# A linear-attention level issued in six steps instead of five, an unscaled k in its last level, and moving sums on VectorE instead of GpSimd

## Chip, core and metric

The kernel runs on one core of a Trainium2 chip. The metric is the device time of one execution in microseconds (us). Engines are named as in the profile: PE (TensorE), PEld (its weight loads), DVE (VectorE), ACT (ScalarE), POOL (GpSimd), SP (which issues most DMAs). Each engine works through its own instructions strictly in order, and waits at an instruction whose inputs are not there.

## What is computed

Two layers of a diffusion backbone over 128 context tokens and 256 latent tokens (T = 384 columns, features on the partitions). Each layer has a projection, three parallel mixers (A: attention, B: gated linear attention, C: a pooling mixer), three gated branch projections, an output projection, and a feed-forward part. The parts that matter here, cut from the reference:

```python
# B, per chunk of 64 tokens: decays between every pair of positions
diff = b_[:, :, :, None, :] - b_[:, :, None, :, :]
decay = jnp.exp(jnp.where(causal, diff, -jnp.inf))
A = jnp.einsum('bhtd,bhsd,bhtsd->bhts', q_, k_, decay)
...
# C, per group of 128 channels with window w = 2, 4, 8, 16
win_sum = cs[:, hi, gi] - cs[:, lo, gi]
pooled = win_sum / cnt - uf
y = jnp.einsum('btgi,gio->btgo', pooled, w_pool)
```

All of it is float32. A product is made of three passes (high times high, low times high, high times low), so every weight tile is split into `wh` (ACT, L151) and `wl` (DVE, L155).

## The kernel before

**Segments and ticks.** The main line is a list of segments, mostly one weight tile times 24 matmuls (`mm3`, L219) into a PSUM bank of `pd` (three banks), evacuated by ACT. Beside it run Python generators, the threads. A segment ticks twice: in the middle of its matmuls and at its end. At a tick every thread issues its instructions up to its next `yield`, in the order in which the threads were started. A tick is a place in the issue order of each engine, not a time; one segment of 24 matmuls lasts about 4.2 us, so a tick about 2.1 us of PE. After the mid-tick the segment issues the `wl` split (L155) of the tile two segments ahead.

**Order in a layer.** Counting ticks from the end of the last row segment (tick 1), a layer's segments are: `uc` 0 to 3 (ticks 2 to 9: mid and end of each), `ka` (10, 11), `va` (12, 13), `q` 0 to 3 (14 to 21), `vb` 0 to 3 (22 to 29, L1353, three banks of `pd` at once), `rb` 0 to 3 (30 to 37), then the gates and weights of branch c (from 38; L1421 are branch matmuls), a and b. L472 are small modulation matmuls between segments.

**Thread B (`gla`).** It makes the gates at ticks 2 to 5 (L726 to L738) and the diagonal at 6 (L771). Then come seven levels with blocks of B = 128, 64, ..., 2 rows. A level has five things to do: `subs` (four DVE subtractions of 128x384, L787 to L790), `exps` (two ACT exponentials of 128x768, L793), `mults` (two DVE products of 128x768, L797: z = 0 for q, z = 1 for k), `products` (small matmuls L762 or L810) and what takes their result out of PSUM: four DVE copies (L817, level 0), eight ACT copies (L825, level 1), or two predicated DVE copies (L832, later levels). They are issued over five ticks: level 0's `subs` at 7 and `exps` at 8 and 9; then `mults` 0 and `subs` 1 at 11 and 12, `exps` 1 at 13 and 14, `products` 0 at 15; `mults` 1, `subs` 2 at 16 and 17, `exps` 2 at 18 and 19, `products` 1 at 20; and so on to `products` 6 at 42. After that the thread waits for the attention, which ends at tick 63.

**Thread C (`pool_mix`).** It starts at tick 9. Per group g it issues on POOL g + 1 additions (L1151, about 410 columns), two multiplications and two subtractions (L1156, L1157, 128 and 256 columns) into the one buffer `pl`, yields four times, and issues the matmul L1161 that reads `pl`, its two evacuations (L1163 ACT, L1164 DVE), and yields again. So the matmuls of groups 0 to 3 stand at ticks 13, 18, 23 and 28. POOL does not wait for ticks and runs ahead up to the reuse of `pl`.

**Thread A (`attn`).** It starts at tick 21; its scores (L1066, DVE L1070 to L1074, ACT L1082 and L1083, DVE L1089 to L1091, transposes L1101, PSUM evacuation L1102, L1112) are issued from tick 33 on. All three threads take their PSUM banks in turn out of four (`psa`); a pair of scores holds two of them until the next tick.

Of the kernel before, what the change touches and what calls it, by code (L numbers as in the profile page):

```python
# [10 lines left out]
AF = mybir.ActivationFunctionType  # L11
ALU = mybir.AluOpType
# [11 lines left out]
LEVELS = (128, 64, 32, 16, 8, 4, 2)  # L24
# [6 lines left out]
class Kern:  # L31
# [683 lines left out]
    def gla_gates(self, l, gl, wg):  # L715
# [3 lines left out]
        yield  # L719
        E = self.mid(8, [128, 4, T])  # L720
        N = self.mid(9, [128, 4, T])
        for q in range(4):
# [4 lines left out]
            b = self.vec[l][:, V_BG + q:V_BG + q + 1]  # L727
            nc.scalar.activation(E[:, q, :], ps, AF.Abs, bias=b)
            nc.vector.tensor_scalar(N[:, q, :], ps, b, 0.0, op0=ALU.add, op1=ALU.min)
# [17 lines left out]
    def gla(self, l, st):  # L747
        nc, P = self.nc, self.P
        qk = st["qbkb"]
        qk2 = qk.rearrange("p (s i) t -> p s (i t)", s=2)  # L750
# [22 lines left out]
        yield  # L773
        lev = {}

        def subs(li):
            B = LEVELS[li]
            W = B // 2
            E = lev[li] = self.mid(8 + li % 2, [128, 2, 768])
            v = lambda x: x.rearrange("p a (n t w) -> p a n t w", t=2, w=W)  # L780
            b = v(P[:, 0:6, 1:129])
            c = v(P[:, 6:12, 0:128])
            rf = b[:, :, :, 0, W - 1:W].to_broadcast([128, 6, 128 // B, W])
            rb = c[:, :, :, 1, 0:1].to_broadcast([128, 6, 128 // B, W])
            qe = v(E[:, 0].rearrange("p (a t) -> p a t", a=6))
            ke = v(E[:, 1].rearrange("p (a t) -> p a t", a=6))
            nc.vector.tensor_tensor(qe[:, :, :, 1], b[:, :, :, 1], rf, op=ALU.subtract)  # L787
            nc.vector.tensor_tensor(ke[:, :, :, 0], rf, b[:, :, :, 0], op=ALU.subtract)
            nc.vector.tensor_tensor(qe[:, :, :, 0], rb, c[:, :, :, 0], op=ALU.subtract)
            nc.vector.tensor_tensor(ke[:, :, :, 1], c[:, :, :, 1], rb, op=ALU.subtract)  # L790

        def exps(li, z):
            nc.scalar.activation(lev[li][:, z], lev[li][:, z], AF.Exp, scale=1.0 / 16)  # L793

        def mults(li):
            for z in range(2):
                nc.vector.tensor_tensor(lev[li][:, z], lev[li][:, z], qk2[:, z], op=ALU.mult)  # L797

        def products(li):
            B = LEVELS[li]  # L800
            E = lev.pop(li)
            Q, K = E[:, 0], E[:, 1]
            if B == 128:
                ps = self.psg()
                for c in range(3):
                    for h in range(4):
                        base = (h // 2) * 384 + c * 128
                        f = (c * 2 + h // 2) * 64
                        for z in range(2):
                            nc.tensor.matmul(  # L810
                                ps[h % 2][64 * z:64 * z + 64, f:f + 64],
                                K[hp(h), base + 64 * z:base + 64 * z + 64],
                                Q[hp(h), base + 64 * (1 - z):base + 64 * (1 - z) + 64],
                                tile_position=(64 * (h % 2), 64 * z))
                for y in range(2):
                    for z in range(2):
                        nc.vector.tensor_copy(  # L817
                            Ap[64 * z:64 * z + 64, y, :, 64 * (1 - z):64 * (1 - z) + 64],
                            ps[y][64 * z:64 * z + 64, 0:384].rearrange("p (a t) -> p a t", t=64))
            elif B == 64:  # L820
                ps = self.psg()
                small(ps, K, Q, True)
                for y in range(2):
                    for j in range(4):
                        nc.scalar.activation(  # L825
                            Ap[32 * j:32 * j + 32, y, :, 32 * (j ^ 1):32 * (j ^ 1) + 32],
                            ps[y][32 * j:32 * j + 32, 0:192].rearrange("p (a t) -> p a t", t=32), AF.Copy)
            else:
                ps = self.psg()
                small(ps, K, Q, False)  # L830
                for z in range(2):
                    nc.vector.copy_predicated(  # L832
                        Dg[:, z * 6:z * 6 + 6], self.masks[:, li - 2].unsqueeze(1).to_broadcast([128, 6, 32]),
                        ps[z][:, 0:192].rearrange("p (a t) -> p a t", t=32))

        NL = len(LEVELS)
        for li in range(NL + 1):
            if li:
                mults(li - 1)
                yield  # L840
            if li < NL:
                subs(li)
                yield
                for z in range(2):
                    exps(li, z)
                    yield
            if li:
                products(li - 1)
            yield
        for j in range(4):  # L850
            nc.vector.tensor_copy(A[32 * j:32 * j + 32, :, 32 * j:32 * j + 32], Dg[32 * j:32 * j + 32])
        while not st.get("attn_done"):
# [39 lines left out]
        for d in range(2):  # L892
            ps = pg[d]
            for n in range(2):
                c = 0 if n == 0 else 1 + d
# [57 lines left out]
        for c in range(3):  # L953
            gc = go[:, c * 4:c * 4 + 4, :]
            nc.vector.tensor_tensor(gc, gc, rs[:, c * 4:c * 4 + 4].unsqueeze(2).to_broadcast([128, 4, 128]),
                                    op=ALU.mult)
# [179 lines left out]
    def pool_mix(self, l, st):  # L1136

        nc = self.nc
        inv = st["inv"]
        wp = st["misc"][:, 512:1024]  # L1140
        och, ocl = st["oc"]
        for g in range(4):
            u = st["uc"][g]
            w = 2 << g
            n = 416
            src = u
            for s in range(g + 1):
                sh = 1 << s
                n -= sh
                dst = st["pw"][s % 2]  # L1150
                nc.gpsimd.tensor_tensor(dst[:, 0:n], src[:, 0:n], src[:, sh:sh + n], op=ALU.add)  # L1151
                src = dst
            pl = self.t("pl", [128, T], bufs=1)
            for (c0, c1), off in zip(SEG, (8, 24)):
                o = off + c0 - w // 2
                nc.gpsimd.tensor_tensor(pl[:, c0:c1], src[:, o:o + c1 - c0], inv[:, g, c0:c1], op=ALU.mult)  # L1156
                nc.gpsimd.tensor_tensor(pl[:, c0:c1], pl[:, c0:c1], u[:, off + c0:off + c1], op=ALU.subtract)  # L1157
            for _ in range(4):
                yield
            ps = self.psa()  # L1160
            nc.tensor.matmul(ps[:, 0:T], wp[:, g * 128:g * 128 + 128], pl)  # L1161
            s = self.vec[l][:, V_PS + g:V_PS + g + 1]
            nc.scalar.activation(och[:, g, :], ps[:, 0:T], AF.Copy, scale=s)  # L1163
            nc.vector.scalar_tensor_tensor(out=ocl[:, g, :], in0=ps[:, 0:T], scalar=s,  # L1164
                                           in1=och[:, g, :].bitcast(F32), op0=ALU.mult, op1=ALU.subtract)
            yield
        st["pool_done"] = True
# [567 lines left out]
```

## Time and profile before

| | us |
|---|---|
| median of 3 runs (1335.37 to 1337.27) | 1336.8 |
| the profiled execution | 1336.65 |
| its span, first to last instruction | 1334.8 |
| around the span | 1.85 |
| PE busy, DVE busy, ACT busy, POOL busy | 1295.1, 857.8, 595.6, 144.4 |
| the B and C threads in layer 0, layer 1 | about 55 to 180, about 711 to 840 |

PE is busy nearly all the time, so only what keeps PE waiting, or slows its clock, counts. The views to read are therefore who PE waited for, then the time lines of the engines around those waits.

### The profile page before, as it was taken

Reading aid. Unit: us, or ns where it says so; the run is one execution under the profiler, and the core shown is the slowest. Engines: PE = TensorE matmul, PEld = TensorE weight load, DVE = VectorE, ACT = ScalarE, POOL = GpSimd, SP = SyncE. Lnnn points to the kernel's source line nnn. Section 1 sums busy time; section 2 is a strip of 40 time slices with the busy share of each in tenths; the row PEclk is TensorE's granted clock in tenths of the full one; section 3 lists DMA queues with packets and bytes.
Section 4 is the critical chain, followed back from the end, with each engine's and each line's share of the span. In section 5 each row is a group of like instructions: output and inputs, shape, how many; then the busy total and the mean of one; then the engine's idle time right before and its main releaser. Section 6 shows DMA issues by size and latency. Waiting matters only on the chain.

```text
span 1334.8 us, 23428 instructions
## 1 busy us (share of the span) xinstructions
PE 1295.1 (97%) x9285; PEld 1201.8 (90%) x9285; DVE 857.8 (64%) x1528; ACT 595.6 (45%) x1104; POOL 144.4 (11%) x190
## 2 busy tenths in 40 slices
PE   7998999999999999999998899999999999999998
PEld 5796788889998999999988777888999899999998
DVE  4497976454568767676877878754556777544432
ACT  5646545343356333332446545543435643333221
POOL 1142000010033000000222500001101300000000
PEclk9999999999999999999999999999999999999999
DMA  9942545557444656565745435456344366444442
GB/s 288 243 113 84 155 120 147 159 135 199 133 126 120 193 168 202 172 204 174 206 133 138 118 97 147 123 149 168 101 124 128 91 190 190 141 127 121 130 131 61
DMA packets 297789, 198.51 MB, mean 149 GB/s; under 512 B 24561, under 2 KB 282385, under 8 KB 297681
## 3 DMA queue, kind: packets, MB, share of 16 engines
q1 hardware_dynamic: 296928, 196.68, 52.3%
q8 instruction: 73, 1.20, 0.4%
q0 software_dynamic: 608, 0.28, 0.1%
q14 instruction: 36, 0.29, 0.1%
q10 hardware_dynamic: 144, 0.07, 0.0%
HBM read 194.64 MB, written 2.36 MB: 148 GB/s over the span
## 4 chain that ended last, share of the span: by engine, by line
PE 81%; DVE 9%; issue 3%; ACT 3%; DMA 2%; SPq 1%; POOL 1%; DVEq 0%; ACTq 0%; POOLq 0%
PE d L219 60%; PE d L1421 8%; DMA m<-in_w_mod_dram 2%; DVE wl L155 2%; PE d L1353 2%; PE m L472 1%; DVE m L797 1%; PE s L1112 1%; PE s L1066 1%; PE s L1101 1%; PE s L941 1%; SPq L1173 1%; DVE ev L656 1%; PE s L935 1%; POOL hl L671 1%
## 5 line engine op out<-in xcount | busy, mean ns | idle before, releaser
L155 DVE TENSOR_TENSOR wl<-raw,wh 128x1024 fp32r<-128x1024 f32 (+2 forms) x274 | 328.6, 1202 | 125.9 <-ACT wh L151 121.6
L151 ACT ACTIVATE wh<-raw 128x1024 fp32r<-128x1024 f32 (+2 forms) x276 | 280.2, 1017 | 173.8 <-PE d L219 63.4
L219 PE MATMUL d<-hh,wh 128*128 128x384 f32 x1248 | 249.3, 343 | 4.0 <-DVE vf L624 2.3
L219 PE MATMUL d<-hl,wh 128*128 128x384 f32 x1248 | 251.2, 340 | 0.0
L219 PE MATMUL d<-hh,wl 128*128 128x384 f32 x1248 | 242.1, 337 | 0.9 <-DVE wl L155 0.8
L219 PEld LDWEIGHTS d<-hh,wh 128*128 128x128 f32 x1248 | 216.9, 189 | 19.9 <-issue 13.9
L219 PEld LDWEIGHTS d<-hh,wl 128*128 128x128 f32 x1248 | 218.4, 188 | 1.9 <-DVE wl L155 1.9
L219 PEld LDWEIGHTS d<-hl,wh 128*128 128x128 f32 x1248 | 217.4, 189 | 1.9 <-issue 0.3
L219 PE MATMUL d<-m,wh 128*128 128x384 f32 x896 | 166.0, 337 | 0.0
L219 PEld LDWEIGHTS d<-m,wh 128*128 128x128 f32 x896 | 155.7, 188 | 0.4 <-issue 0.4
L251 ACT ACTIVATE m<-tt 128x384 fp32r<-128x384 f32 x60 | 31.3, 525 | 157.6 <-DVE tt L1523 125.6
L219 PE MATMUL d<-m,wl 128*128 128x384 f32 x448 | 87.5, 336 | 0.0
L219 PEld LDWEIGHTS d<-m,wl 128*128 128x128 f32 x448 | 78.6, 189 | 0.0
L1421 PE MATMUL d<-m,wh 128*128 128x384 f32 x384 | 72.2, 341 | 0.0
L1421 PEld LDWEIGHTS d<-m,wh 128*128 128x128 f32 x384 | 66.0, 188 | 6.6 <-issue 5.8
L710 DVE SCALAR_TENSOR_TENSOR x<-d,modT,x 128x128 f32<-128x128 f32 x64 | 23.6, 413 | 54.8 <-PE d L219 47.0
L1441 POOL TENSOR_TENSOR m<-m,tt 128x384 f32<-128x384 f32 x16 | 17.0, 1081 | 366.7 <-DVE tt L1439 366.7
L561 POOL TENSOR_TENSOR ssq<-ssq,ev 128x384 f32<-128x384 f32 x18 | 29.5, 1636 | 249.3 <-ACT ev L559 249.3
L1404 ACT ACTIVATE tt<-d 128x384 f32<-128x384 f32 x48 | 23.6, 491 | 70.8 <-PE d L219 60.9
L1523 DVE TENSOR_TENSOR tt<-tt,d 128x384 f32<-128x384 f32 x42 | 23.3, 554 | 48.9 <-PE d L219 48.6
L1510 ACT ACTIVATE tt<-d 128x384 f32<-128x384 f32 x42 | 20.6, 491 | 64.9 <-PE d L219 60.9
L498 DVE SCALAR_TENSOR_TENSOR A<-raw,sc,A 128x1024 f32<-128x1024 f32 x35 | 47.1, 1345 | 0.0
(317 smaller groups left out, 1595.4 us busy)
## 6 DMA issues: line engine op xcount, KB each, us to landing
raw<-in_w_mod_dram SPq DMA_DIRECT2D x80, 512.0 KB, 3.8
raw<-in_w_in_dram SPq DMA_DIRECT2D x76, 512.0 KB, 4.0
raw<-in_w_ff_gate_dram SPq DMA_DIRECT2D x44, 512.0 KB, 4.9
raw<-in_w_ff_up_dram SPq DMA_DIRECT2D x44, 512.0 KB, 4.3
raw<-in_w_ff_down_dram SPq DMA_DIRECT2D x32, 448.0 KB, 4.4
m<-in_w_mod_dram SPq DMA_DIRECT2D x16, 512.0 KB, 6.9
raw<-in_w_in_dram SPq DMA_DIRECT2D x32, 256.0 KB, 3.8
raw<-in_w_out_dram SPq DMA_DIRECT2D x16, 512.0 KB, 4.0
```

The costliest lines, as they stand in the source:

```text
L151: nc.scalar.activation(h[:, f], w[:, f], AF.Copy)
L155: e.tensor_tensor(l[:, f], w[:, f], h[:, f].bitcast(F32), op=ALU.subtract)
L219: nc.tensor.matmul(ps, w[:, k * width + col:k * width + col + 128], xs[xi](k0 + k), start=first and n == 0, stop=last and n == tot - 1)
L251: self.nc.scalar.activation(h, v, AF.Copy)
L498: nc.vector.scalar_tensor_tensor(out=acc, in0=self.raw[u], scalar=s, in1=acc, op0=ALU.mult, op1=ALU.add)
L561: e.tensor_tensor(self.ssq, self.ssq, sq, op=ALU.add)
L710: nc.vector.scalar_tensor_tensor(out=self.x[n][:, c0:c1], in0=ps[:, c0:c1], scalar=self.modT[l][:, fg + n, v:v + 1], in1=self.x[n][:, c0:c ...
L1353: nc.tensor.matmul(vps[c], (self.hl if z else self.hh)[kk][:, c * 128:c * 128 + 128], w[:, k * 512:k * 512 + 512], start=kk == 0 and w is ...
L1404: nc.scalar.activation(tt, ps[:, 0:T], AF.Tanh, scale=0.5)
L1421: nc.tensor.matmul(ps[i], w[:, k * 256 + i * 128:k * 256 + i * 128 + 128], x2[xi](k), start=w is h and xi == 0 and k == 0, stop=w is lo an ...
L1510: nc.scalar.activation(tt, pg, AF.Tanh, scale=0.5)
L1523: nc.vector.tensor_tensor(tt, tt, pu, op=ALU.mult)
```

## The change

The six steps of a level are now: `mults` z = 0, `mults` z = 1, `subs` z = 0, `subs` z = 1 together with the `products` of the level before, `exps` 0, `exps` 1. Each of the two `mults` and the two halves of `subs` has a tick of its own. Level 0 runs over ticks 7 to 10; `products` 0 to 6 stand at ticks 14, 20, 26, 32, 38, 44 and 49. At B = 2 the k side (whose exponent is zero) takes no `subs`, `exps` or `mults`, and `products` reads k as it is. In the pooling thread the additions, multiplications and subtractions go to DVE, with a yield after every second addition and two yields instead of four ahead of the matmul: the matmuls L1161 stand at ticks 11, 15, 19 and 24.

```diff
-        def subs(li):
+        def subs(li, z):
...
-            E = lev[li] = self.mid(8 + li % 2, [128, 2, 768])
+            if z == 0:
+                lev[li] = self.mid(8 + li % 2, [128, 2, 768])
+            elif W == 1:
+                return
...
+            e = v(lev[li][:, z].rearrange("p (a t) -> p a t", a=6))
+            if z == 0:
+                nc.vector.tensor_tensor(e[:, :, :, 1], b[:, :, :, 1], rf, op=ALU.subtract)
+                nc.vector.tensor_tensor(e[:, :, :, 0], rb, c[:, :, :, 0], op=ALU.subtract)
+            else:
+                nc.vector.tensor_tensor(e[:, :, :, 0], rf, b[:, :, :, 0], op=ALU.subtract)
+                nc.vector.tensor_tensor(e[:, :, :, 1], c[:, :, :, 1], rb, op=ALU.subtract)
...
         def exps(li, z):
-            nc.scalar.activation(lev[li][:, z], lev[li][:, z], AF.Exp, scale=1.0 / 16)
-
-        def mults(li):
-            for z in range(2):
+            if z == 0 or LEVELS[li] > 2:
+                nc.scalar.activation(lev[li][:, z], lev[li][:, z], AF.Exp, scale=1.0 / 16)
+
+        def mults(li, z):
+            if z == 0 or LEVELS[li] > 2:
                 nc.vector.tensor_tensor(lev[li][:, z], lev[li][:, z], qk2[:, z], op=ALU.mult)
...
-            Q, K = E[:, 0], E[:, 1]
+            Q, K = E[:, 0], E[:, 1] if B > 2 else qk2[:, 1]
...
         for li in range(NL + 1):
-            if li:
-                mults(li - 1)
+            for z in range(2 if li else 0):
+                mults(li - 1, z)
                 yield
-            if li < NL:
-                subs(li)
+            for z in range(2 if li < NL else 0):
+                subs(li, z)
+                if z:
+                    break
                 yield
-                for z in range(2):
-                    exps(li, z)
-                    yield
             if li:
                 products(li - 1)
             yield
+            for z in range(2 if li < NL else 0):
+                exps(li, z)
+                yield
...
-                nc.gpsimd.tensor_tensor(dst[:, 0:n], src[:, 0:n], src[:, sh:sh + n], op=ALU.add)
+                nc.vector.tensor_tensor(dst[:, 0:n], src[:, 0:n], src[:, sh:sh + n], op=ALU.add)
                 src = dst
+                if s % 2:
+                    yield
...
-                nc.gpsimd.tensor_tensor(pl[:, c0:c1], src[:, o:o + c1 - c0], inv[:, g, c0:c1], op=ALU.mult)
-                nc.gpsimd.tensor_tensor(pl[:, c0:c1], pl[:, c0:c1], u[:, off + c0:off + c1], op=ALU.subtract)
-            for _ in range(4):
+                nc.vector.tensor_tensor(pl[:, c0:c1], src[:, o:o + c1 - c0], inv[:, g, c0:c1], op=ALU.mult)
+                nc.vector.tensor_tensor(pl[:, c0:c1], pl[:, c0:c1], u[:, off + c0:off + c1], op=ALU.subtract)
+            for _ in range(2):
                 yield
```

## Rows read from the trace of the kernel before

**Rows 1.** The page, part 1: busy us (share of the span) and instructions.

```profile
PE 1295.1 (97%) x9285; PEld 1201.8 (90%) x9285; DVE 857.8 (64%) x1528; ACT 595.6 (45%) x1104; POOL 144.4 (11%) x190
```

**Rows 2.** Waits of PE, whole span: line, releaser: us in total, times, longest.

```profile
PE d L1353 <- ACT m L1333: 9.5, 3, 4.7
...
PE s L1066 <- ACT pr L1083: 2.7, 2, 1.4
...
PE d L219 <- ACT m L1365: 1.7, 2, 0.8
```

**Rows 3.** Time line of ACT, both layers: start, us, line, count, idle before, releaser.

```profile
99.99 0.84 ACT L793 ACTIVATE m<-m 128x768 f32<-128x768 f32 x1 [4.92 <-DVE m L789]
...
103.72 2.63 ACT L825 ACTIVATE A<-s 32x192 f32<-32x192 f32 x8
...
756.22 0.85 ACT L793 ACTIVATE m<-m 128x768 f32<-128x768 f32 x1 [7.37 <-DVE m L789]
```

**Rows 4.** Time line of PE in and after the first `vb` segment, both layers.

```profile
107.37 2.08 PE L1353 MATMUL d<-wh,hh 128*128 128x512 f32 x4 [3.66 <-ACT m L1333]
109.25 2.08 PE L1353 MATMUL d<-wh,hl 128*128 128x512 f32 x6
...
123.30 1.56 PE L1353 MATMUL d<-wl,hh 128*128 128x512 f32 x6
...
763.60 2.07 PE L1353 MATMUL d<-wh,hh 128*128 128x512 f32 x4 [4.66 <-ACT m L1333]
765.47 2.76 PE L1353 MATMUL d<-wh,hl 128*128 128x512 f32 x6
```

**Rows 5.** Busy by stretch: us, PE, PEld, DVE, ACT, POOL, PEclk, DMA, GB/s.

```profile
757.00:775.00 18.00, 12.15 (x44) 7.66 (x43) 9.71 (x13) 11.21 (x23) 5.47 (x6) 0.81 0.31 88
```

**Rows 6.** Time lines of DVE (alone, then beside POOL) and POOL, layer 1.

```profile
730.76 0.56 DVE L789 TENSOR_TENSOR m<-P 128x384 f32<-128x384 f32 x1
...
741.00 1.23 DVE L789 TENSOR_TENSOR m<-P 128x384 f32<-128x384 f32 x1
...
740.62 3.49 POOL L1151 TENSOR_TENSOR m<-m 128x415 f32<-128x415 f32 x3
```

**Rows 7.** DVE groups by form, 60 to 120 us: busy, mean ns, idle before.

```profile
L155 DVE TENSOR_TENSOR wl<-raw,wh 128x1024 fp32r<-128x1024 f32 x11 | 16.5, 1500 | 3.0 <-ACT wh L151 2.9
L797 DVE TENSOR_TENSOR m<-m,m 128x768 f32<-128x768 f32 x6 | 7.0, 1201 | 0.0
...
L790 DVE TENSOR_TENSOR m<-P 128x384 f32<-128x384 f32 x4 | 3.3, 820 | 0.0
```

**Rows 8.** A DVE group of 256 columns, 60 to 145 us.

```profile
L979 DVE TENSOR_TENSOR ev<-ev,m 128x256 f32<-128x256 f32 x5 | 2.1, 427 | 0.2
```

**Rows 9.** Time lines of DVE and PE around ticks 9 to 11, layer 0, then layer 1.

```profile
77.42 0.17 DVE L422 TENSOR_SCALAR nsink<-sink 128x16 f32<-128x16 f32 x1
...
77.04 1.55 PE L219 MATMUL d<-hh,wl 128*128 128x384 f32 x8
...
721.04 3.20 DVE L738 TENSOR_TENSOR_SCAN P<-cst,m 128x128 f32<-128x128 f32 x6
...
726.26 2.00 DVE L738 TENSOR_TENSOR_SCAN P<-cst,m 128x128 f32<-128x128 f32 x6
...
731.70 1.23 DVE L155 TENSOR_TENSOR wl<-raw,wh 128x1024 fp32r<-128x1024 f32 x1
...
729.97 1.66 PE L219 MATMUL d<-hh,wl 128*128 128x384 f32 x8
```

**Rows 10.** Time lines of PE and DVE at the first scores, layer 0.

```profile
141.48 0.92 PE L1066 MATMUL s<-KA,m 64*128 64x384 f32 x4
...
149.67 1.75 PE L1066 MATMUL s<-KA,m 64*128 64x384 f32 x4 [1.38 <-ACT pr L1083]
...
152.36 2.74 PE L219 MATMUL d<-hh,wh 128*128 128x384 f32 x8
...
146.01 0.29 DVE L1070 TENSOR_TENSOR s<-s,amask 128x128 f32<-128x128 f32 x1
```

More of the change, by code (lines that the diff above doesn't have):

```diff
@@ L784, in subs @@
             rb = c[:, :, :, 1, 0:1].to_broadcast([128, 6, 128 // B, W])
[L785 to L790, printed above, removed]
+            e = v(lev[li][:, z].rearrange("p (a t) -> p a t", a=6))
[5 more added lines that the diff above has]
+                nc.vector.tensor_tensor(e[:, :, :, 1], c[:, :, :, 1], rb, op=ALU.subtract)
         def exps(li, z):
-            nc.scalar.activation(lev[li][:, z], lev[li][:, z], AF.Exp, scale=1.0 / 16)
-        def mults(li):
-            for z in range(2):
+            if z == 0 or LEVELS[li] > 2:
+                nc.scalar.activation(lev[li][:, z], lev[li][:, z], AF.Exp, scale=1.0 / 16)
+        def mults(li, z):
+            if z == 0 or LEVELS[li] > 2:
                 nc.vector.tensor_tensor(lev[li][:, z], lev[li][:, z], qk2[:, z], op=ALU.mult)
```

## The prediction, made before the changed kernel was run

> **What bounds the kernel.** I read the page's busy times first: PE is busy for 97% of the span [rows 1], so time can only come from what keeps PE waiting or slows it. Next the waits of PE. The largest is the first `vb` segment (L1353) waiting for ACT to evacuate `q` 3 (L1333): 9.5 us in three waits over the two layers. Then come the scores behind L1083 (2.7 us) and `rb` 0 behind L1365 (1.7 us) [rows 2]. The time line of ACT shows why L1333 is late: ACT stands idle for 4.92 and 7.37 us ahead of one exponential, until DVE has finished the `subs` of that level, and has then to catch up on evacuations, splits and the eight copies L825 [rows 3]. The waits cost more than their length, because PE comes out of them slow: six `vb` matmuls take 2.08 and 2.76 us against 1.56 undisturbed [rows 4], and the granted clock is 0.81 over that stretch of layer 1 [rows 5], part of it at the lower of the clock's two levels. DVE, last, is late for two reasons that the rows show. A tick drops four subtractions or two products on it at once. And it runs slowly beside POOL: the same subtraction takes 0.56 us alone and 1.23 us while POOL makes its additions [rows 6].
>
> **Part 1, the pooled sums on DVE.** Per layer 26 instructions move: 10 additions of some 410 columns, 8 of 128 and 8 of 256. Rows give 0.427 us for 256 columns [rows 8] and 0.56 for 384 [rows 6], so 0.13 per 128 columns: 0.59 for an addition, 0.30 for 128 columns. Each needs the one before, so I take whole durations: group 0 costs 0.59 + 2 x 0.30 + 2 x 0.43 = 2.05 us, groups 1 to 3 one addition more each (2.64, 3.23, 3.82), together 11.7 us. No row shows this exact shape on DVE. From below it can't be less than nothing, from above I take POOL's own price, 3.49 us for three additions, 1.16 each [rows 6], twice mine; my value follows the nearer DVE rows. In return DVE is rid of POOL: from 60 to 120 us the 11 splits L155 average 1.50 against 1.23 alone [rows 7, 9], 3.0 us; six products L797 average 1.20 against an estimated 0.95 (0.56 + 3 x 0.13), 1.5 us; L790 0.82 against 0.56, 1.0 us in four, its sister lines up to as much: 5.5 to 8.5 us a layer.
>
> The Trainium skill speaks for and against here. Its page "SBUF — State Buffer", section "Who interferes with whom", says that a DVE instruction with two SBUF inputs contends with a GpSimd instruction that reads SBUF; the 0.56 and 1.23 agree. "Perfetto Trace Analysis", section "Optimizing Scalar/DVE Operations", advises to take work off a saturated DVE, even to GpSimd. By that rule the whole of this part would land on the path, which is the second rival below.
>
> What is new is who waits. The L1161 of a group now stands two ticks (4.2 us of PE) behind DVE's work for it, and PE waits there with every later matmul behind it.
> Group 0, layer 0 (ticks 9 to 11): DVE comes free at 77.6 (end of L422, which precedes it at tick 9) and is done at 79.65; PE ends `ka` at 77.04 + 1.55 = 78.6 [rows 9]. Wait: 1.1 us.
> Group 0, layer 1: DVE ends the split at 731.70 + 1.23 = 732.9. It gets there 1.2 us sooner, since six of the scans before it took 3.20 beside POOL against 2.00 for the other six [rows 9]: 731.7 + 2.05 = 733.8. PE ends `ka` at 729.97 + 1.66 = 731.6 [rows 9]. Wait: 2.2 us, which may bring slow matmuls; 0 to 2.2 us by what the longer waits cost (below), taken as 1.0.
> Groups 1 and 2 (up to tick 19): DVE has to do four splits (4.9), three products (2.85), 11 pieces of about 0.56 (four subtractions, seven copies and evacuations; 6.2) and the pooled 2.64 + 3.23, in all 19.8 us from 79.65, some 1 us less where starts overlap. PE has four segments, 16.6 us, and 2.4 of small matmuls, 19.0 from 79.7. They tie: 0 to 0.7 us of waiting, taken as 0.3 a layer. Group 3 (tick 24) has `vb` 0 ahead of it, where DVE has the least to do: 9.71 us busy of 18 [rows 5]. Nothing.
>
> **Part 2, six steps.** Every step still costs the same instructions. ACT's `exps` now come one tick or more behind the last of their `subs`, and at ticks 17 to 20 ACT has none to wait for, so the idle 4.92 and 7.37 us go. What is late next at `vb` 0 is the eight copies L825: `products` 1 is at tick 20 as before, ACT then needs 2.63 [rows 3] and two evacuations of about 0.5 each, 3.7 us, while PE has half of `q` 3 and two matmuls, 2.6 us. Wait that stays: 1.1 us a layer.
> Before: layer 0 waits 3.66 and is slow for (2.08 - 1.04) + (2.08 - 1.56) = 1.5 us [rows 4], 5.2 together; layer 1 waits 9.5 - 3.66 = 5.9 [rows 2, 4] and is slow for (2.07 - 1.04) + (2.76 - 1.56) = 2.2 [rows 4], 8.1.
> After: layer 0 1.1 + 0.3 + 1.1 = 2.5; layer 1 2.2 + 1.0 + 0.3 + 1.1 = 4.6. **Gain 2.7 + 3.5 = 6.2 us.**
> L1365: the exponential ahead of it, at tick 28, now has its `subs` two ticks behind it, so ACT is free for the copy; of the 1.7 us [rows 2] I take 1.4.
>
> The scores: before, `products` 4 (tick 35) took the two free PSUM banks, and the scores of that tick waited for an exponential of ACT. Layer 0 lost 1.38, 0.83 on slow scores (1.75 against 0.92) and 1.1 on a slow segment (2.74 against 1.66) [rows 9, 10], 3.3; layer 1 the rest of the 2.7 [rows 2] and the same slow scores, 2.1. `products` 4 now stands at tick 38, with two banks held by scores, so the transpose L1101 behind it must wait until DVE has read the products (L832). PE waits there for as long as DVE is behind. Before, DVE reached the first scores at 146.01, 3.6 us behind PE (141.48 + 0.92) [rows 10]. It now has 3.0 us less to do by then (two subtractions and two products later) and starts a tick (2.1) later: 2.7 behind. Over the next four ticks it has 1.7 us less than before. I take a wait of 2 us a layer; bounds 0.4 (DVE not behind) and 5. **Gain 5.4 - 4.0 = 1.4.** `products` 5 and 6 keep such waits, small before and after.
>
> **Part 3, no k side at B = 2.** Two subtractions (1.1), one product (0.95) on DVE and one exponential (0.85 [rows 3]) on ACT fall away per layer, at ticks 43 to 48. PE waits for neither there: nothing. The seven extra ticks end at 50, thirteen before the attention for which the thread then waits: nothing. The cover is those thirteen ticks; without it each tick would cost 2.1 us.
>
> **Sum.** 6.2 + 1.4 + 1.4 = 9.0 us. The profiled execution, 1336.65 (span 1334.8 and 1.85 around it), becomes 1327.65; the median lay 0.15 above it: **1327.8 us**, 0.67% faster. What a measurement here can tell from no change is about 0.2%, 2.7 us.
>
> **Rivals.**
> *The scores give it back.* PE arrives sooner at ticks 33 to 38, and if DVE stays 3.6 us behind, the wait for L832 is 4 us a layer, with 2 us of slow matmuls as after the 1.38 [rows 10]: 12 us in place of 5.4, that is 9.0 - 1.4 - 6.6 = 1.0 us gained, **1335.8**. For it: DVE's work up to there is packed. Against it: less of that work is due before tick 38.
> *DVE is the bound up to tick 19.* In that stretch DVE and PE tie, so each microsecond more on DVE is one of PE waiting at L1161, in both layers. Groups 0 to 2 cost 7.9 us a layer by my price. At POOL's price, twice that, 15.8 us go against 9.0: **1343.6**, slower. It decides from 9.0 / 2 = 4.5 us more a layer, 1.57 times my price; so too if DVE's slow pieces (5.5 to 8.5 us) were not POOL's doing and stayed. Against it: subtractions take 0.56 whenever POOL rests [rows 6].
> *The early waits don't come* and DVE has caught up by tick 38: 1.1 + 0.3 + 2.2 + 1.0 + 0.3 and 3.2 of the 4 us fall away, **1319.7**.
> *The idle ACT was not the cause*, and `vb` 0 still waits 9.5 us and comes out slow (13.3 before, 2.2 in the sum): 9.0 - 11.1, **1338.9**, no change. L825 ahead of L1333 speaks for it, the idle 4.92 and 7.37 against.
>
> **How the numbers follow.** Forecast 0.52, scores 0.15, DVE bound 0.14, early waits absent 0.12, ACT not the cause 0.07. Forecast and absent waits are faster (0.64); the scores' case lies astride the limit (0.07 faster, 0.08 same); the last is mostly the same (0.05, slower 0.02); DVE as the bound is slower (0.13) or, just past its turning point, the same (0.01). Faster 0.71, same 0.14, slower 0.15. The range takes in the absent waits and the scores' case: 1318 to 1339.
>
> **What would show it.** Right: in ACT's time line no idle time of over 2 us ahead of L793; L1353's wait for L1333 near 1.1 us, twice; new waits of PE L1161 near 1 and 2 us for DVE at group 0; L787 to L790 near 0.56 throughout; a wait of L1101 for L832 near 2 us at tick 38. Wrong: waits of L1161 at groups 1 and 2, pooled additions on DVE well over 0.6 us, or L1101 waiting 4 us or more.

## The result, and the profile of the changed kernel

The changed kernel takes **1328.4 us** (median of 4 runs, 1326.68 to 1329.97) against 1336.9 for the kernel before in the same session: ratio 0.9941, 95% interval 0.9925 to 0.9956, so 8.5 us or 0.6% faster. Forecast was 1327.8. The profiled execution took 1327.16 us with a span of 1325.3, 9.5 less than the span before.

Lines move by some ten: `subs` are L791 to L795, `exps` L799, `mults` L803, the products L762, L816 and their copies L823, L831, L838, the scores L1074 with L1091, the transposes L1109, the pooled sums L1159 to L1167 and their matmul L1171, `vb` L1363 behind L1343, `rb` behind L1375.

The page's busy times, in answer to [rows 1]: DVE has 1.4 us more, POOL 53 less.

```profile
PE 1291.1 (97%) x9285; PEld 1200.7 (91%) x9285; DVE 859.2 (65%) x1574; ACT 595.7 (45%) x1102; POOL 91.8 (7%) x138
```

The waits of PE over the span (line, releaser: us in total, times, longest), in answer to [rows 2]. The 9.5 us behind L1333 are 1.8, and the 1.7 us of `rb` are gone from the list. The waits L1171 for the pooled sums and L762 are new, and L1109 for the products waits longer than before (the last line is that wait in the kernel before, four times 0.4 us). The scores' wait is almost what it was (2.4 against 2.7).

```profile
PE s L1171 <- DVE pl L1167: 2.6, 2, 1.6
PE s L1109 <- DVE Dg L838: 2.6, 4, 1.4
PE s L1074 <- ACT pr L1091: 2.4, 2, 1.2
...
PE d L1363 <- ACT m L1343: 1.8, 2, 0.9
...
PE s L762 <- DVE m L252: 1.0, 2, 0.5
```

```profile
PE s L1101 <- DVE Dg L832: 1.6, 4, 0.4
```

The same waits in PE's time line (start, us, then idle before and releaser in brackets), first layer 0, then layer 1; they answer to [rows 4] and [rows 10]. The four and six `vb` matmuls behind the wait run at full speed (1.19 and 1.56, before 2.08 and 2.08), but behind the scores' wait at 151.86 a segment is slow (2.61 for eight matmuls that take 1.66 undisturbed). Around that wait the two scores of the pair run one after the other, 0.91 us each, where both together take 0.92 undisturbed (at 162.20); so the scores lose some 0.9 us beside their wait, in both layers.

```profile
79.93 0.91 PE L1171 MATMUL s<-pl,m 128*128 128x384 f32 x2 [0.99 <-DVE pl L1167]
...
106.82 1.19 PE L1363 MATMUL d<-wh,hh 128*128 128x512 f32 x4 [0.91 <-ACT m L1343]
107.85 1.56 PE L1363 MATMUL d<-wh,hl 128*128 128x512 f32 x6
...
149.78 0.91 PE L1074 MATMUL s<-KA,m 64*128 64x384 f32 x2
151.86 0.91 PE L1074 MATMUL s<-KA,m 64*128 64x384 f32 x2 [1.16 <-ACT pr L1091]
...
153.27 2.61 PE L219 MATMUL d<-hh,wh 128*128 128x384 f32 x8
...
158.51 0.55 PE L1109 MATMUL s<-ident,pr 128*128 128x128 f32 x3 [0.40 <-DVE Dg L838]
...
162.20 0.92 PE L1074 MATMUL s<-KA,m 64*128 64x384 f32 x4
...
730.58 0.91 PE L1171 MATMUL s<-pl,m 128*128 128x384 f32 x2 [1.64 <-DVE pl L1167]
...
757.48 1.20 PE L1363 MATMUL d<-wh,hh 128*128 128x512 f32 x4 [0.92 <-ACT m L1343]
...
802.59 0.91 PE L1074 MATMUL s<-KA,m 64*128 64x384 f32 x2 [1.23 <-ACT pr L1091]
...
808.72 0.55 PE L1109 MATMUL s<-ident,pr 128*128 128x128 f32 x3 [1.41 <-DVE Dg L838]
```

DVE's groups from 60 to 120 us (busy us, mean ns of one, idle before), in answer to [rows 7]. Splits take 1217 ns instead of 1500, products 951 instead of 1201, subtractions 552 instead of 820.

```profile
L155 DVE TENSOR_TENSOR wl<-raw,wh 128x1024 fp32r<-128x1024 f32 x11 | 13.4, 1217 | 0.3 <-ACT wh L151 0.3
L803 DVE TENSOR_TENSOR m<-m,m 128x768 f32<-128x768 f32 x6 | 5.6, 951 | 0.0
...
L791 DVE TENSOR_TENSOR m<-P 128x384 f32<-128x384 f32 x4 | 2.2, 552 | 0.0
```

The first pooled addition in DVE's time line (0.59 us); the longest idle time of ACT ahead of an exponential up to `vb` (1.22 us, in answer to [rows 3]); and the stretch of [rows 5] (us, PE, PEld, DVE, ACT, POOL, granted clock, DMA share, GB/s). There PE is busy 17.52 of 18 us instead of 12.15, at a granted clock of 1.00 instead of 0.81. The stretch is the same by the clock, not instruction for instruction.

```profile
77.84 0.59 DVE L1159 TENSOR_TENSOR m<-m 128x415 f32<-128x415 f32 x1
```

```profile
726.59 1.28 ACT L799 ACT_TABLE_LOAD   x1 [1.22 <-DVE m L792]
```

```profile
757.00:775.00 18.00, 17.52 (x172) 13.00 (x173) 11.88 (x28) 11.32 (x14) 0.00 (x0) 1.00 0.28 86
```

### The profile page after: what moved, and what is told of

It is laid out like the page before. It is cut to its first block, busy times and chain, and to the rows that moved or that the text cites. A ratio compares the mean times of both kernels' runs of the same rounds, so it can differ in the third digit from the quotient of the medians.

```text
span 1325.3 us, 23398 instructions
## 1 busy us (share of the span) xinstructions
PE 1291.1 (97%) x9285; PEld 1200.7 (91%) x9285; DVE 859.2 (65%) x1574; ACT 595.7 (45%) x1102; POOL 91.8 (7%) x138
## 4 chain that ended last, share of the span: by engine, by line
PE 85%; DVE 6%; DMA 3%; issue 2%; ACT 2%; SPq 1%; POOL 1%; ACTq 0%; POOLq 0%; DVEq 0%
PE d L219 62%; PE d L1431 7%; PE d L1363 3%; DMA m<-in_w_mod_dram 2%; PE m L472 2%; DVE wl L155 1%; PE s L1120 1%; PE s L1074 1%; DMA raw<-in_w_in_dram 1%; PE s L1109 1%; PE s L762 1%; PE s L949 1%; DVE ev L656 1%; PE s L943 1%; POOL hl L671 1%
## 5 line engine op out<-in xcount | busy, mean ns | idle before, releaser
L155 DVE TENSOR_TENSOR wl<-raw,wh 128x1024 fp32r<-128x1024 f32 (+2 forms) x274 | 325.0, 1189 | 126.9 <-ACT wh L151 122.9
L151 ACT ACTIVATE wh<-raw 128x1024 fp32r<-128x1024 f32 (+2 forms) x276 | 280.0, 1017 | 179.3 <-PE d L219 64.2
```

The source lines that it names most:

```text
L151: nc.scalar.activation(h[:, f], w[:, f], AF.Copy)
L155: e.tensor_tensor(l[:, f], w[:, f], h[:, f].bitcast(F32), op=ALU.subtract)
```

## Experiments

Theory: PE waits at `vb` 0 because ACT stands idle for `subs` and then catches up; six steps remove that, and the pooled sums on DVE pay for themselves. Rivals: only one of the two parts gains; or DVE is the bound somewhere and hands the gain back. Medians in us, ratio to the kernel before measured beside each:

| steps, pooling, products 4 to 6 | us | ratio, 95% |
|---|---|---|
| before: five, POOL, ticks 35 to 42 | 1336.9 | 1 |
| changed: six, DVE, ticks 38 to 49 | 1328.4 | 0.9925 to 0.9956 |
| six, POOL, ticks 38 to 49 | 1326.5 | 0.9910 to 0.9935 |
| five, DVE, ticks 35 to 42 | 1336.2 | 0.9986 to 1.0003 |
| six, DVE, ticks 42 to 53 | 1323.2 | 0.9891 to 0.9918 |
| six, POOL, ticks 42 to 53 | **1319.1** | 0.9853 to 0.9883 |
| five, POOL, ticks 42 to 49 | 1341.3 | 1.0022 to 1.0047 |

**The engine of the pooled sums alone.** The changed kernel, with its ticks, and additions, multiplications and subtractions on POOL.

```diff
-                nc.vector.tensor_tensor(dst[:, 0:n], src[:, 0:n], src[:, sh:sh + n], op=ALU.add)
+                nc.gpsimd.tensor_tensor(dst[:, 0:n], src[:, 0:n], src[:, sh:sh + n], op=ALU.add)
...
```

> The changed kernel with one thing undone: the pooled additions, multiplications and subtractions are back on POOL, at the new ticks. Theory A (the spread of a level over six steps is what gains; the pooled work on DVE and the slowdown beside POOL weigh about the same): the subtractions of the levels average 0.7 us or more again before 120 us, the waits of L1171 for its input change but stay under 3 us in all, no idle time of ACT over 2 us ahead of the exponentials between 90 and 105 us, and the time stays within 3 us of the changed kernel, 1326 to 1331. Theory B (taking POOL's work away is what gains, through the freed DVE): DVE falls behind again, the first vb segment waits 5 us or more in the two layers together, and the time is 1333 or more.

Measured: 1329.5 us, ratio 0.9935 to 0.9960, not to be told from the changed kernel. PE waits once, in layer 0, for POOL (time line of PE), and DVE's subtractions are slow again (groups of DVE in layer 0):

```profile
82.32 1.65 PE L1171 MATMUL s<-pl,m 128*128 128x384 f32 x2 [3.05 <-POOL pl L1167]
```

```profile
L792 DVE TENSOR_TENSOR m<-P 128x384 f32<-128x384 f32 x3 | 3.2, 1059 | 0.0
```

Subtractions of 1.06 us on average in place of 0.55 show in none of PE's waits: in this run DVE has slack enough up to tick 24, as long as PE doesn't wait for its pooled sums.

**Each part alone.** First the six steps and the unscaled k, with the pooling thread as it was (the diff); then the five steps, with the pooling thread of the change (the same lines the other way round, in the kernel before).

```diff
-                nc.vector.tensor_tensor(dst[:, 0:n], src[:, 0:n], src[:, sh:sh + n], op=ALU.add)
+                nc.gpsimd.tensor_tensor(dst[:, 0:n], src[:, 0:n], src[:, sh:sh + n], op=ALU.add)
                 src = dst
-                if s % 2:
-                    yield
...
-            for _ in range(2):
+            for _ in range(4):
```

> The levels' part alone (six steps, no k side at B = 2), with the pooling thread wholly as before: on POOL, four yields. Theory A: no wait of PE for pl at all, the first vb segment waits about 1 us in each layer as in the changed kernel, and the time is that of the changed kernel or up to 3 us less: 1325 to 1329. Theory B (the freed DVE is needed): the vb waits of before remain for the larger part, 1333 or more.

> The pooling part alone (on DVE, its new yields), with the levels in five steps as before. Theory A: ACT again stands idle for 3 us or more ahead of an exponential whose subtractions come one tick earlier, and the first vb segment waits 2 us or more in each layer; with the new waits for pl (2 to 3 us in all) the time is 1333 to 1338. Theory B: the subtractions take 0.56 us, DVE is on time and the vb waits are gone; 1326 to 1330.

Measured: 1326.5 and 1336.2 us. The steps alone bring 10.4 us, no less than the whole change; the pooled sums on DVE bring nothing that can be told. Waits of PE in the first, then a group of its DVE from 60 to 120 us:

```profile
PE s L1109 <- DVE Dg L838: 5.4, 4, 2.7
...
PE d L1361 <- ACT m L1341: 1.8, 2, 0.9
```

```profile
L791 DVE TENSOR_TENSOR m<-P 128x384 f32<-128x384 f32 x4 | 3.4, 856 | 0.0
```

The `vb` wait goes although subtractions stay slow (856 ns): the new order is enough, without POOL's share. What PE no longer loses to L1171 it loses in part at tick 38 (5.4 us instead of 2.6). The second kernel's waits of PE:

```profile
PE s L1163 <- DVE pl L1159: 8.3, 4, 3.2
...
PE d L1355 <- ACT m L1335: 1.8, 2, 0.9
```

Here I had expected two microseconds or more a layer to stay at `vb`, behind an ACT that stands idle for 3 us or more; neither came, though the time did (1333 to 1338). The lost time has moved: PE now stops 8.3 us for `pl`, two groups a layer, and so comes to `vb` when ACT has caught up. ACT itself is hardly earlier. Its exponential of level 2 starts 0.8 and 0.5 us sooner than before [rows 3], although the subtractions ahead of it take 0.55 us again:

```profile
99.22 0.84 ACT L793 ACTIVATE m<-m 128x768 f32<-128x768 f32 x1 [1.94 <-DVE m L789]
...
755.71 0.84 ACT L793 ACTIVATE m<-m 128x768 f32<-128x768 f32 x1 [1.41 <-DVE m L789]
```

The wait that disappears is no proof of its cause.

**The pooled work twice.** The changed kernel with each addition and multiplication issued a second time, 5.7 us more on DVE per layer up to tick 19 and 3.1 more for group 3.

```diff
+                nc.vector.tensor_tensor(dst[:, 0:n], src[:, 0:n], src[:, sh:sh + n], op=ALU.add)
...
                 nc.vector.tensor_tensor(pl[:, c0:c1], src[:, o:o + c1 - c0], inv[:, g, c0:c1], op=ALU.mult)
+                nc.vector.tensor_tensor(pl[:, c0:c1], src[:, o:o + c1 - c0], inv[:, g, c0:c1], op=ALU.mult)
```

> The changed kernel with every pooled addition and multiplication issued twice on DVE (18 more instructions per layer, 5.7 us more of DVE's work up to tick 19, 3.1 more for group 3). Theory, as predicted (DVE and PE tie up to tick 19, so each microsecond more on DVE is a microsecond of PE waiting for pl): L1171 waits 1.3 us longer at group 0 and for most of the rest at groups 1 and 2, 12 to 16 us in all over both layers against 2.6, and the time is 8 to 13 us more, 1336 to 1342. Rival (DVE has slack there): the waits grow by the 1.3 us of group 0 only, and the time by 3 us or less.

Measured: 1341.6 us, ratio 1.0025 to 1.0055, so slower than before and 13.2 us over the changed kernel, a little beyond what I expected. Its waits of PE:

```profile
PE s L1173 <- DVE pl L1169: 11.4, 4, 3.6
```

Up to tick 19 both layers get 11.4 us more of DVE's work, and the waits for `pl` grow by 8.8 (from 2.6). L1109 waits 1.8 us more (4.4 against 2.6), and the rest of the 13.2 isn't taken apart here. So DVE and PE do tie up to tick 19: the rival that put DVE there as the bound had the right place, and about three quarters of its rate show as waits. Only the price of an addition (0.59, not 1.16) kept it from happening.

**A tick more ahead of each pooled matmul, and the eight copies later.** Two attempts on the waits that the change leaves: three yields in place of two ahead of L1171, and the copies L831 issued behind the evacuation of `q` 3.

```diff
-            for _ in range(2):
+            for _ in range(3):
                 yield
```

> The changed kernel with three yields instead of two ahead of the pooled matmul, so that it stands three ticks behind DVE's work. Theory A (the waits for pl, 0.99 and 1.64 us in the changed kernel, are waits at one place and not a bound): they vanish, nothing new comes in their place, 2 to 3 us less than the changed kernel, 1325 to 1327. Rival (DVE is the bound up to tick 19): PE saves the wait and loses it at the products or at the later pooled matmuls, since DVE has the same work to do; no change against the changed kernel, 1327 to 1330.

```diff
-                for y in range(2):
-                    for j in range(4):
-                        nc.scalar.activation(
+                def out():
+                    for y in range(2):
+                        for j in range(4):
+                            nc.scalar.activation(
...
+                self.late.append(out)
```

> The changed kernel with the eight ACT copies of products 1 issued behind the evacuation of q 3 instead of ahead of it. Theory (those copies are what is left of the wait at the first vb segment): L1363 no longer waits for L1343 (0.91 and 0.92 us in the changed kernel). Whether the 1.8 us reach the end depends on the next stage: if DVE is the bound between ticks 25 and 38, they return as longer waits at the second scores or behind products 4, and the time is that of the changed kernel, 1327 to 1329; if not, 1326 to 1327.

Measured: 1327.2 (0.9908 to 0.9935) and 1327.6 us (0.9925 to 0.9950), 1.3 us and 0.8 us less, neither to be told from the changed kernel. Waits of PE, first with three yields, then with the copies later:

```profile
PE s L1109 <- DVE Dg L838: 6.3, 4, 2.8
PE s L1171 <- DVE pl L1167: 1.1, 1, 1.1
```

```profile
PE s L1112 <- DVE Dg L841: 4.2, 4, 1.9
...
PE d L1366 <- ACT m L1346: 1.2, 2, 0.6
```

Both take the wait aimed at (2.6 to 1.1, and 1.8 to 1.2: the copies explain a third of what is left at `vb`, not all of it as I had it). With three yields PE loses it again at tick 38 (6.3 instead of 2.6). For the copies that isn't shown: a rise from 2.6 to 4.2 also comes without any change ahead of tick 38, as the run with k scaled below shows.

Up to tick 38 DVE has hardly a pause. In layer 1 of the changed kernel it goes from 767.18 to L838 at 808.29 with a single one, of 0.80 us, and PE waits 1.41 us for it:

```profile
795.08 1.23 DVE L155 TENSOR_TENSOR wl<-raw,wh 128x1024 fp32r<-128x1024 f32 x1 [0.80 <-ACT wh L151]
...
808.29 0.64 DVE L838 COPY_PREDICATED Dg<-masks,s 128x192 f32<-128x192 uint8 x2
```

There an earlier PE only waits longer (2.7 us with three yields). In layer 0 of the same trace DVE is on time: before L838 it waits 0.32 us itself, for the products, behind PE's wait at the scores and the slow matmuls after it.

**The last levels later.** The changed kernel with four empty ticks, so that products 4 to 6 stand at ticks 42, 48 and 53.

```diff
             for z in range(2 if li < NL else 0):
                 exps(li, z)
                 yield
+            for _ in range(4 if li == 4 else 0):
+                yield
```

> The changed kernel with four empty ticks between the exponentials of level 4 and its products, so that some 4.7 us of DVE's work for the levels (two mults, four subs, the copies of products 4) moves past tick 38; products 4 to 6 stand at ticks 42, 48 and 53, still ahead of the attention's end. Theory (between ticks 25 and 38 DVE has more to do than PE, and whatever PE saves earlier it waits for there): the waits at the second scores and behind products 4, 2.6 and 2.6 us in the changed kernel with L762's and the slow matmuls behind them, fall to under 2 us in all, and the time is 3 to 5 us less than the changed kernel, 1323 to 1326. Rival (the score wait comes from ACT, which is held up by a late weight transfer, not from DVE's lag): the waits of L1074 for L1091 stay above 2 us, 1327 to 1330.

Measured: **1323.2 us**, 0.9891 to 0.9918. Its waits of PE:

```profile
PE s L1173 <- DVE pl L1169: 4.2, 2, 3.2
...
PE s L1111 <- DVE Dg L838: 1.6, 4, 0.4
PE s L1076 <- ACT pr L1093: 1.5, 2, 0.8
```

L838 is back at the 0.4 a time that it had before the change; with it the scores and L838 still wait 3.1 us, where I had expected under 2. The gain of 5.2 us is measured, its cause is argued: the four ticks take some 4.7 us of DVE's work from ahead of tick 38, but they also put the products at other ticks among the attention's scores and transposes, and no run separates the two.

**k scaled again at B = 2.** The changed kernel with the k side computed at the last level.

```diff
...
-            Q, K = E[:, 0], E[:, 1] if B > 2 else qk2[:, 1]
+            Q, K = E[:, 0], E[:, 1]
```

> The changed kernel with the k side at B = 2 computed as before (two subs, one exps, one mults more per layer, about 2.0 us of DVE and 0.85 us of ACT). Theory: they lie at ticks 43 to 48, where PE waits for neither engine; no change against the changed kernel, 1326.5 to 1330. Rival (DVE is short there too, and products 5 or 6 come late): 2 us or more slower, 1330 and over, with L762 or L1109 waiting longer.

Measured: 1329.5 us, 0.9938 to 0.9963, against 0.9925 to 0.9956 for the changed kernel: no difference that can be told. Up to tick 38 its instructions are those of the changed kernel, and yet its trace waits differently there:

```profile
PE s L1107 <- DVE Dg L836: 4.5, 4, 1.9
...
PE s L1072 <- ACT pr L1089: 1.3, 2, 0.7
```

At tick 38 it waits 1.92 and 1.83 us, at the scores 0.65 and 0.66, where the changed kernel's trace has 0.40 and 1.41, and 1.16 and 1.23. So one trace doesn't fix how a loss of this size divides between neighbouring waits.

**Putting the pieces together.** The six steps, the later levels and the pooling thread as it was on POOL, which joins two edits shown above; then the same levels with pooling on DVE and one yield more in group 0 (the diff).

```diff
...
-            for _ in range(2):
+            for _ in range(3 if g == 0 else 2):
```

> The six steps and the unscaled k, with products 4 to 6 moved to ticks 42, 48 and 53, and the pooling thread as before, on POOL. Theory A (six steps carry the gain, products past the scores carry the next 5 us, and DVE between the pooled sums and tick 38 is the bound): the kernel with the levels alone took 1326.5 us and waited 5.4 us for L838; with the levels moved, most of that goes, as it did in the changed kernel (1328.4 to 1323.2): 1320 to 1323 us, no wait over 1.5 us behind DVE's L838. Theory B (POOL's slowdown of DVE, 0.74 to 0.86 us a subtraction instead of 0.55, eats it): 1324 to 1327 us, L838 waits over 3 us.

> The changed kernel with products 4 to 6 at ticks 42, 48 and 53, and the matmul of group 0 one tick later (12 instead of 11), the other groups as they are relative to it. Theory A: the kernel with the later levels alone (1323.2) still waits 4.2 us for pl at L1171 (1.0 and 3.2); one tick of PE, 2.1 us, covers the first and most of the second: 1319 to 1322 us, L1171 waits under 1.5 us. Theory B (what PE gains there returns as waits later in the stretch, as in the kernel with three yields alone): 1322.5 to 1325 us, and the wait stands again at L838 or at a later L1171.

Measured: **1319.1** and **1320.6 us** (0.9865 to 0.9892), both faster than the kernel before and the changed one, the first by a microsecond more than its theory had. Waits of PE in the first: no pooled matmul is among them.

```profile
PE d L1363 <- ACT m L1343: 1.8, 2, 0.9
PE s L1111 <- DVE Dg L838: 1.6, 4, 0.4
PE s L1076 <- ACT pr L1093: 1.1, 2, 0.8
```

With the levels spread and late, moving the pooled sums to DVE, at their earlier ticks, costs 4 us (1323.2 against 1319.1), which one more tick of cover for group 0 mostly returns. The Trainium skill, page "Perfetto Trace Analysis", section "Optimizing Scalar/DVE Operations", doubts that moving work between DVE and GpSimd helps, and says that breaking up instructions may let work finish sooner where an engine isn't saturated but causes bubbles on others. The first agrees with these runs: moving the pooled sums is worth nothing to minus 4 us. To the second they are only near: no instruction was broken up here, the same ones were issued in smaller groups, and that brought 10 us.

**The later levels without the six steps.** The kernel before, with seven empty ticks ahead of the products of level 4 (ticks 42, 47 and 49). Then the same with the exponentials L1085 of the first two pairs of scores issued right behind the scores.

```diff
+            for _ in range(7 if li == 4 else 0):
+                yield
```

> The kernel before, five steps and the pooling on POOL, with seven empty ticks ahead of the products of level 4, so that products 4 to 6 stand at ticks 42, 47 and 49. Theory A (the waits of vb 0 and those of the scores are two separate losses): the scores' loss of 5.4 us goes in part, vb 0 waits its 9.5 us as before: 1332 to 1335 us. Theory B (the later place of the products alone carries the gain, and the six steps only happened to bring it about): 1325 to 1329 us, with the vb wait much shorter.

```diff
-            if s % 2 and s <= n:
+            if s % 2 and 3 < s <= n:
...
                 score(s)
                 score(s + 1)
+                if s < 3:
+                    expo(s)
+                    expo(s + 1)
```

> The kernel before with the products of level 4 and later moved (1341.3 us), and in it the exponentials L1085 of the first two pairs of scores issued right behind the scores, at ticks 33 and 35 instead of 34 and 36, so that on ACT they stand ahead of the split L151 that waits for its weight tile. Theory A (the scores at tick 37 wait because the exponential that frees their PSUM bank stands behind that L151): the two waits of 3.3 and 3.4 us and the slow matmuls behind them (2.5 us a layer) go: 1331 to 1335 us. Theory B (the exponential is late because DVE is late with the scores): the waits stay at 2 to 3.5 us, and ACT now holds L151 back too: 1340 to 1344 us.

Measured: 1341.3 us (1.0022 to 1.0047) and 1340.6 (1.0018 to 1.0037), both slower than before. The first lies outside both of its theories (its `vb` wait is still 9.1 us), the second where its rival put the time, though not for the rival's reason. In the first, PE waits 3.33 us at the scores of tick 37. On ACT the exponential that frees their bank stands behind a split that waits for its weight tile; DVE in turn waits for that split. From the time lines, by start: two splits on ACT, the DVE split between them, and PE:

```profile
150.14 1.06 ACT L151 ACTIVATE wh<-raw 128x1024 fp32r<-128x1024 f32 x1 [5.15 <-DMA raw<-in_w_in_dram]
...
151.23 1.23 DVE L155 TENSOR_TENSOR wl<-raw,wh 128x1024 fp32r<-128x1024 f32 x1 [2.78 <-ACT wh L151]
...
156.57 1.06 ACT L151 ACTIVATE wh<-raw 128x1024 fp32r<-128x1024 f32 x1 [3.32 <-DMA raw<-in_w_in_dram]
...
158.51 1.11 PE L1068 MATMUL s<-KA,m 64*128 64x384 f32 x2 [3.33 <-ACT pr L1085]
```

With the exponentials early, that wait is gone, and one of the same size stands a tick or two later, behind the next exponential and the next weight tile:

```profile
161.66 1.06 ACT L151 ACTIVATE wh<-raw 128x1024 fp32r<-128x1024 f32 x1 [4.37 <-DMA raw<-in_w_br_c_dram]
...
163.99 1.55 PE L1114 MATMUL s<-pT,vt 128*64 128x128 f32 x12 [3.31 <-ACT pr L1085]
```

By these lines what is late there is the weight stream, not DVE's work on the scores; no run changes the stream alone. In the first of the two kernels the split L155 frees a weight buffer (ends at 152.46), SP issues the next tile at 152.48, and L151 starts at 156.57, 4.1 us later. Splits L151 come 6.0 to 6.6 us apart (at 143.55, 150.14, 156.57, 162.55), while a segment of `rb` takes PE 5.8. The same chain is in the changed kernel: its scores' wait at 151.86 ends with an exponential that starts at 151.06, right behind the split in the line below (in layer 1 the split at 800.64 waits 2.81 us, and the scores at 802.59 follow). It was there before the change too: the exponential that ends the wait in [rows 10] stands behind a split that waited 1.61 us for its tile, with an exponential of the levels between them.

```profile
149.91 1.06 ACT L151 ACTIVATE wh<-raw 128x1024 fp32r<-128x1024 f32 x1 [2.72 <-DMA raw<-in_w_in_dram]
```

Why the same later levels gain 7.4 us with six steps and lose 4.3 with five isn't settled by a run of its own. In the best kernel the splits come at 136.14, 142.12 and 147.77, closer together (5.98 and 5.65). A fifth weight buffer would test the chain directly; no run has one.

## Why the prediction was right, point by point

Terms of the sum, in us, against the profiled execution:

| what is left to wait (layer 0; layer 1) | predicted | measured |
|---|---|---|
| group 0 for DVE, with slow clock | 1.1; 3.2 | 0.99; 1.64 |
| groups 1 and 2 | 0.3; 0.3 | 0; 0 |
| `vb` 0 | 1.1; 1.1 | 0.91; 0.92 |
| `rb` 0, both layers | 0.3 | 0 |
| scores, tick 37: wait, divided pair, slow matmuls | 0; 0 | 3.7; 2.1 |
| tick 38, L1109 | 2; 2 | 0.40; 1.41 |
| products 6, tick 49 | 0; 0 | 0.5; 0.5 |

**What bounds, and the cause at `vb` 0**: right. In ACT's time line the largest idle time ahead of L799 up to `vb` is 1.22 us (before 4.92 and 7.37 [rows 3]), the wait is 0.9 twice, and the slow matmuls behind it are gone. The run with the steps alone shows that this is the six steps' doing. They change several things at once (a tick for each product and each half of the subtractions, later exponentials, later products); the later products alone, with five steps, gain nothing (1341.3), and the rest no run takes apart. Of the 0.9 that stay only 0.3 were the eight copies.

**Pooled price**: right (0.59 for an addition). The time given back by POOL is there too: 11 splits at 1217 ns instead of 1500 are 3.1 us, as costed. What was wrong is its worth: with the steps in the new order, DVE's faster pieces bought nothing on the path, while L1171's new waits cost. In the sum both stood inside one term, so the error doesn't show in the total: I gave part 1 and part 2 one common gain of 6.2, and 9.0 with `rb` and the scores, where the steps alone bring 10.4 and the pooling alone 0.7, within its interval of no change.

**Group 0 in layer 1** was too dear: 1.64 instead of 2.2, and no slow clock behind it, 1.6 us less.

**The scores** were the term that failed by its mechanism. I put the whole loss at tick 38, behind DVE's L838, since two PSUM banks are held there. Tick 38 does wait, but 0.4 and 1.41 in this trace (1.92 and 1.83, near my 2, in the one with k scaled). The old wait for an exponential, which I had leave with products 4, stayed one tick earlier, at 1.16 and 1.23, with 0.9 for the divided pair in each layer and 1.6 us of slow matmuls in layer 0 (2.61 - 1.66, and 0.6 in the four behind them). Without the slow matmuls the scores lose 2.1 us a layer, as before (1.38 and 1.27 of waiting, 0.83 each on the scores themselves): the change freed nothing there. Nor were those 0.83 us slow matmuls, as I read them: the granted clock over them is 0.98 and 1.00, and in layer 0 the weight load of the second score waits 0.54 us for a second exponential. The cause of the wait isn't products 4, which now come later: transposes and the next pair of scores use the four banks up as well, and in the time lines the exponential that would free one stands behind a split waiting for its weight tile. In sum 7.6 against 4.0 predicted.

**Seven extra ticks at nothing**: not quite. L762 waits 0.5 us a layer at tick 49. That the extra ticks as such cost something isn't seen: moving the levels four ticks later still gains 5.2 us.

**k at B = 2**: nothing, as predicted, and shown by computing it again.

So that the total came out to 0.6 us is luck in part. Too much at group 0 (1.7), at groups 1 and 2 (0.6) and at `vb` and `rb` (0.7) stood against too little at the scores (3.6) and at products 6 (1.0). The terms measured leave 13.1 of the 20.4 us that the prediction counted as lost before (13.3, 1.7 and 5.4): a gain of 7.3, where the span is 9.5 shorter. By layers it is plainer: the prediction's terms give 4.7 us in layer 0 and 4.3 in layer 1, PE's time lines show 2.9 and 6.6. In layer 0 the measured terms account for the 2.9. In layer 1 they leave some 2 us that were not forecast; two smaller waits of the kernel before (0.9 us at L1112, 0.8 for L155) are no longer in the list of waits, and the rest isn't taken apart. What was not luck is the largest term, `vb` 0.

## What to carry to other kernels

Where an engine issues in order, look first at what stands ahead of the late instruction, and only then at how long the late one takes: issuing a level in six steps instead of five gained 10 us, while making its subtractions a third faster by taking POOL's work away gained nothing. A wait that goes away because its engine arrives later is only moved; look whether what it waited for really comes sooner. When gains keep coming back as waits at one place, find the engine that has no pause up to there, and try to move work off it that isn't due yet: that gained 5.2 us and more with six steps, and lost 4.3 with five, so it has to be tried.

## What the runs showed that was not expected

A wait of the same length is not always followed by slow matmuls. Before layer 1's projections PE waits 2.0 us for `vf` (L624) in the changed kernel and in the one with the later levels. The window of the changed kernel that holds the wait (us, PE, PEld, DVE, ACT, POOL, granted clock, DMA share, GB/s) is this; in the other kernel the granted clock is 1.00 in this window, which there begins right behind the wait:

```profile
700.00:710.00 10.00, 8.02 (x33) 6.91 (x32) 7.70 (x17) 7.99 (x17) 1.54 (x14) 0.83 0.87 261
```

The matmuls right behind the wait, first of the changed kernel, then of the other:

```profile
702.56 2.35 PE L219 MATMUL d<-hh,wh 128*128 128x384 f32 x8 [1.98 <-DVE vf L624]
```

```profile
699.67 1.63 PE L219 MATMUL d<-hh,wh 128*128 128x384 f32 x8 [1.96 <-DVE vf L624]
```

The first has matmuls at the lower clock level and loses some 1.6 us to it (from the end of the wait to the segment's third pass 5.74 us against 4.15); in the trace of the kernel before, the same place ran at 1.00, behind 2.31 us. Seven of the fourteen traces show the lower level there, so a difference of a microsecond or two between single traces can come from this place alone. A term for slow clock behind a wait of 1 to 2 us is a range from nothing to about 1.6 us, not a number.

DVE beside POOL is slowed by less than a whole addition. Subtractions of 0.55 us take 0.67 to 1.06 on average from 60 to 120 us in the runs with POOL's additions there; single ones take up to 1.23 [rows 6], and 1.41 once, in the run that puts the changed kernel's pooled sums back on POOL. The Trainium skill, page "SBUF — State Buffer", section "Who interferes with whom", calls the shared port pair an exclusive lock. A subtraction that had to wait out a whole addition of 1.16 us [rows 6] would take 1.7 us, and none does; but POOL's additions are slowed beside DVE as well (0.91 each in that run while DVE stands idle), and a wait for the rest of one that has begun would fit these rows. So they don't tell how the two share it.
